# Loading and splitting the first two chunks of u at the point where the dense tokens are loaded

## Chip, core and metric

One NeuronCore of a Trainium2 chip runs the whole program in one launch. The metric is the device time in microseconds (us). The kernel before took 2869.16 us (median of three runs, 2865.69 to 2877.17).

## What is computed

One residual block on x of shape 1024 tokens by 1024, in float32. The part that matters here is its last third, the product-key expert layer:

```python
q = (xt @ w_query).reshape(T, 8, 2, 128)
s = einsum('thpd,hpkd->thpk', q, sub_keys)       # scores, 8 heads x 2 x 128 keys
# top 16 of each half, top 16 of their sums -> idx (T, 8, 16), gate = softmax
a = gelu(einsum('td,thkd->thk', xb, expert_u[idx]))
out = einsum('thk,thkd->td', a * gate, expert_v[idx])
```

There are 16384 experts, rows of u and v of 1024 numbers each. Ahead of it stand an RMS norm, the mLSTM and gMLP mixers and an output projection.

## The kernel before

**Two kinds of tokens.** The 1024 tokens are 8 blocks of 128. Blocks 0 to 4 are "dense": all 16384 experts are evaluated for them by matmuls, 128 chunks of 128 experts, and a matrix G holds the gate of each expert and token (zero for most). Blocks 5 to 7 are "sparse": for each of a token's 128 picked experts a row of u, later of v, is gathered by an indirect DMA that POOL issues, and DVE does a dot product or a weighted sum.

**The front.** `front_part` runs three times, over blocks 0-1, 2-4 and 5-7. Its last step is eight calls of `query` (L419): a weight load and split (`split_w`), 48 matmuls into `pq`, their copy on ACT, 12 matmuls of scores (`psc`, L444), and a store of the scores to DRAM that ACT's queue issues (L447, `d_sc<-sc`). The top-k steps load them back on SP's queue (L464, `scb<-d_sc`). Between these stand the gate units of the dense blocks (`gate_units`): DVE builds one-hot tiles `AB` (L656), ACT scales them (L659), PE multiplies them into `pG` (L661), ACT copies that to `Gt` (L662), and ACT's queue stores it to `d_G`.

**open_x.** In the third part, ahead of the eight queries, `open_x` (L738, called at L628) closes the pool of the mixers and opens the pool `xparts` in its place, at the right end of SBUF. It loads the dense tokens `xh` and `xl` (ten loads of 512 KB, L748). `xparts` also holds two buffers for raw chunks of u and v.

**The dense phase.** `experts` opens the pool `dense` where the pool of the front lay, so its tiles wait for the tiles of the front that they overlap. `stage1` takes a chunk of u: load to `raw` (L777), ACT copies it to `uhi` rounded to fp32r (L778), POOL subtracts to get `ulo` (L779). Then `mm3` does three matmuls (hi by hi, hi by lo, lo by hi) for each of 8 slices and each of two half-chunks of 320 tokens: 24 matmuls into one of three PSUM buffers `pa`. ACT takes the GELU (L787), DVE multiplies by the gates `Gin` (L789), ACT and DVE split into `wh` and `wl` (L790, L791), and only then is the `pa` buffer free. `Gin` is loaded once for four chunks (L771, 1280 KB). After four chunks `stage2` splits four chunks of v (L800 to L802), multiplies into `pout` and adds to `acc` (L816).

**Where a raw chunk goes.** `raw()` counts its calls. Until `experts` sets `dense_phase`, every raw tile comes from `xparts`; after that, calls number 1, 4, 5, 8, 9, ... come from the pool `dense`. So before the change the raw tile of chunk 0 lies in `dense`, those of chunks 1 and 2 in `xparts`, that of chunk 3 in `dense`.

**Order.** The code is written in program order, but a list scheduler with a simulated timeline decides the order of each engine's and queue's instructions: it takes the earliest in program order of those that it thinks are ready. Each engine and each queue then runs in that fixed order.

Of the kernel before, what the change touches and what calls it, by code (L numbers as in the profile page):

```python
# [7 lines left out]
F32 = mybir.dt.float32  # L8
F32R = mybir.dt.float32r
# [3 lines left out]
AF = mybir.ActivationFunctionType  # L13
OP = mybir.AluOpType
# [27 lines left out]
SLOW = 0  # L42
ORDER = [0, 1, 4, 2, 3, 5, 6, 7]
SPREAD = 0.96


class Build:
# [690 lines left out]
    def open_x(self):  # L738

        nc = self.nc  # L740
        self.cm.close()
        self.xp = self.ctx.enter_context(self.tc.tile_pool(name="xparts", bufs=1, side="right", reuse_waits="tile"))
        T = len(self.dense) * 128
        self.xh = self.xp.tile([128, 8, T], F32R, name="xh", tag="xh")
        self.xl = self.xp.tile([128, 8, T], F32R, name="xl", tag="xl")
        for s, blk in enumerate(self.dense):
            for src, dst in ((self.d_xh, self.xh), (self.d_xl, self.xl)):
                nc.sync.dma_start(dst[:, :, s * 128:(s + 1) * 128].bitcast(F32), src[blk])  # L748

    def raw(self):  # L750
        self.nraw += 1
        if self.dense_phase and self.nraw % (2 + NRAW2) < NRAW2:
            return self.dp.tile([128, D], F32, name="raw", tag="raw", bufs=NRAW2)
        return self.xp.tile([128, D], F32, name="raw", tag="raw", bufs=2)

    def experts(self, side, dp, ps):
        nc, v = self.nc, self.nc.vector
        self.dense_phase = True
        self.dp = dp
        xh, xl = self.xh, self.xl  # L760
        ND = len(self.dense)
        T = ND * 128
        T2 = T // 2
        n32 = T // TG
        ngroups = NEXP // GS
        W, V, st = {}, {}, {"n": 0}

        def stage1(g, e):
            if e == 0:
                st["G"] = dp.tile([128, n32, GS, TG], F32, name="Gin", tag="Gin", bufs=1)  # L770
                nc.sync.dma_start(st["G"], self.d_G[:, :, g * GS:(g + 1) * GS].rearrange("n j i t -> j n i t"))  # L771
            G = st["G"]
            i = g * GS + e
            ur = self.raw().rearrange("p (c j) -> p c j", c=8)
            ul = dp.tile([128, 8, 128], F32R, name="ulo", tag="ulo", bufs=2)
            uh = dp.tile([128, 8, 128], F32R, name="uhi", tag="uhi", bufs=2)
            nc.sync.dma_start(ur, self.I["uT"][i])  # L777
            nc.scalar.activation(uh, ur, AF.Copy)  # L778
            nc.gpsimd.tensor_tensor(ul, ur, uh.bitcast(F32), op=OP.subtract)  # L779
            wh = dp.tile([128, T], F32R, name="wh", tag="wh", bufs=GS + 1)  # L780
            wl = dp.tile([128, T], F32R, name="wl", tag="wl", bufs=GS + 1)
            for s in range(2):
                pa = ps.tile([128, T2], F32, name="pa", tag="pa", bufs=3)
                sl = slice(s * T2, (s + 1) * T2)
                self.mm3(pa, [((uh[:, c], ul[:, c]), (xh[:, c, sl], xl[:, c, sl])) for c in range(8)])
                with self.first():
                    nc.scalar.activation(pa, pa, AF.Gelu_apprx_tanh)  # L787
                    p3 = pa.rearrange("p (n t) -> p n t", t=TG)
                    v.tensor_tensor(p3, p3, G[:, s * (n32 // 2):(s + 1) * (n32 // 2), e], op=OP.mult)  # L789
                    nc.scalar.activation(wh[:, sl], pa, AF.Copy)  # L790
                    v.tensor_sub(wl[:, sl], pa, wh[:, sl].bitcast(F32))  # L791
            W[i] = (wh, wl)

        def stage2(g):
            vhs, vls = (self.gp.tile([128, GS, D], F32R, name=n, tag="Gt", bufs=2) for n in ("vhi", "vlo"))
            for e in range(GS):
                i = g * GS + e
                vr = self.raw()
                vh, vl = vhs[:, e], vls[:, e]
                nc.sync.dma_start(vr, self.I["v"][i * 128:(i + 1) * 128])  # L800
                nc.scalar.activation(vh, vr, AF.Copy)  # L801
                nc.gpsimd.tensor_tensor(vl, vr, vh.bitcast(F32), op=OP.subtract)  # L802
                V[i] = (vh, vl)
            for s in range(ND):
                for d in range(2):
                    if st["n"] % 3 == 0:
                        po = ps.tile([128, 512], F32, name="pout", tag="pout", bufs=1)
                    else:
                        po = self.gps.tile([128, 512], F32, name="pout", tag="pG", bufs=2)
                    st["n"] += 1  # L810
                    dl = slice(d * 512, (d + 1) * 512)
                    sl = slice(s * 128, (s + 1) * 128)
                    self.mm3(po, [((W[i][0][:, sl], W[i][1][:, sl]), (V[i][0][:, dl], V[i][1][:, dl]))
                                  for i in range(g * GS, (g + 1) * GS)])
                    with self.first():
                        v.tensor_add(st["acc"][:, s, dl], st["acc"][:, s, dl], po)  # L816

        for f in side:
            f()
        units = []  # L820
        for n in range(len(self.sparse)):
            steps = self.sparse_units(self.sparse[n], dp, ps)
            more = [f for b in self.sparse[n + 1:n + 2] for f in self.topk_units(b)]
            for q, f in enumerate(steps):
                units.append(f)
                if q % 20 == 19 and more:
                    units.append(more.pop(0))
            units += more
        last = units.pop()
        k = 0  # L830
        for g in range(ngroups):
            for e in range(GS):
                stage1(g, e)
                i = g * GS + e - LAG
                want = min(len(units), int(len(units) * (i + 1) / (SPREAD * (NEXP - LAG))))
                while k < want:
                    units[k]()
                    k += 1
            if g == 0:
                acc = dp.tile([128, ND, D], F32, name="acc", tag="acc")  # L840
                for s, blk in enumerate(self.dense):
                    nc.sync.dma_start(acc[:, s], self.d_x1[blk])
                st["acc"] = acc
            stage2(g)
        self.fg = dp.tile([128, D], F32, name="fgrow", tag="Gin", bufs=1)
        nc.sync.dma_start(self.fg, self.I["fg"].partition_broadcast(128))
        for s, blk in enumerate(self.dense):
            self.final(blk, acc[:, s], dp)
        for f in units[k:] + [last]:
            f()  # L850
# [148 lines left out]
```

## Time and profile before

| | us |
|---|---|
| median of three runs | 2869.16 |
| profiled execution, its own time | 2870.66 |
| profiled execution, first to last instruction (span) | 2868.9 |
| PE busy, of the span | 2707.1 (94%) |
| DVE busy | 2198.3 (77%) |
| POOL busy | 1498.8 (52%) |
| ACT busy | 1120.5 (39%) |

Matmul ends are modelled, so a busy PE is not a PE at its peak: counts and starts of matmuls tell its pace. The front ends and the dense phase begins at about 973 us of the span. In a timeline row, "0.42 PE ... [3.23 <-DVE acc L816]" means that the engine stood idle 3.23 us before this and that acc, written at line 816 on DVE, ended the wait. PE is the matmuls, PEld the weight loads beside them, SPq and ACTq the DMA queues of those engines.

### The profile page before, as it was taken

The numbers are of one execution on the slowest core, as the hardware profiler recorded it, in microseconds if no ns is written. First come the engines' busy times: TensorE is split into PE (matmuls) and PEld (weight loads), VectorE is DVE, ScalarE is ACT, GpSimd is POOL, SyncE is SP. The second block draws the span as 40 slices with busy tenths as digits, with TensorE's granted clock in tenths as the row PEclk, the third lists the DMA queues.
The fourth block names the chain that finished last, engine by engine and source line by source line (L and its number), as shares of the span: only waits on it lengthen the run. The fifth ranks groups of instructions, "written<-read, shape, count | busy, mean of one in ns | idle before, by whom it ended". The sixth has DMA issues, their size and how long they took to land.

```text
span 2868.9 us, 44783 instructions
## 1 busy us (share of the span) xinstructions
PE 2707.1 (94%) x16283; PEld 2468.9 (86%) x16283; DVE 2198.3 (77%) x4981; ACT 1120.5 (39%) x2295; POOL 1498.8 (52%) x1220
## 2 busy tenths in 40 slices
PE   7888989999898799999999999999999999999998
PEld 7887989889898798889888888888888898889987
DVE  6649975289985677888797787978987777777774
ACT  5444788348888322223222222222222222222222
POOL 4430020000200186767767677667767777777873
PEclk9989999999999899999999999999999999999999
DMA  7797557866578798988989999898989999999992
GB/s 252 253 315 281 187 216 278 277 223 226 186 274 312 257 328 299 335 313 311 326 282 331 338 322 330 300 344 302 316 284 342 343 330 332 331 322 326 336 320 111
DMA packets 327821, 838.41 MB, mean 292 GB/s; under 512 B 25520, under 2 KB 161072, under 8 KB 315824
## 3 DMA queue, kind: packets, MB, share of 16 engines
q0 software_dynamic: 114048, 427.87, 40.4%
q1 hardware_dynamic: 190544, 347.91, 37.0%
q10 hardware_dynamic: 23008, 59.77, 5.3%
q8 instruction: 128, 2.10, 0.3%
q14 instruction: 93, 0.76, 0.1%
HBM read 746.32 MB, written 89.13 MB: 291 GB/s over the span
## 4 chain that ended last, share of the span: by engine, by line
PE 58%; DVE 19%; DMA 9%; ACT 5%; issue 5%; POOL 3%; SPq 1%; ACTq 1%; another core or an unknown queue 0%; POOLq 0%; DVEq 0%
PE pa L96 8%; PE pa L94 7%; PE pa L95 7%; PE pout L94 7%; PE pout L95 7%; PE pout L96 7%; DMA Gin<-d_G 4%; DVE gat L697 2%; PE pG L661 2%; DVE sacc L713 2%; DVE AB L656 2%; PE pq L94 2%; PE pq L96 2%; PE pq L95 2%; DMA wraw<-win 1%
## 5 line engine op out<-in xcount | busy, mean ns | idle before, releaser
L94 PE MATMUL pa<-xh,uhi 128*128 128x320 f32 x2048 | 639.3, 312 | 28.9 <-ACT uhi L778 14.9
L95 PE MATMUL pa<-xl,uhi 128*128 128x320 f32 x2048 | 637.1, 311 | 0.0
L96 PE MATMUL pa<-xh,ulo 128*128 128x320 f32 x2048 | 625.5, 311 | 5.4 <-POOL ulo L779 5.4
L94 PE MATMUL pout<-vhi,wh 128*128 128x512 f32 x1280 | 505.4, 400 | 23.0 <-DVE acc L816 11.1
L713 DVE SCALAR_TENSOR_TENSOR sacc<-gat,aw,sacc 128x1024 f32<-128x1024 f32 x384 | 492.3, 1282 | 27.4 <-DMA gat<-v,ix 22.3
L95 PE MATMUL pout<-vlo,wh 128*128 128x512 f32 x1280 | 509.0, 399 | 0.0
L96 PE MATMUL pout<-vhi,wl 128*128 128x512 f32 x1280 | 490.2, 398 | 0.0
L709 POOL DMA_INDIRECT gat<-v,ix x384 | 363.5, 947 | 239.8 <-DVE sacc L713 131.0
L697 DVE SCALAR_TENSOR_TENSOR gat<-gat,xn 128x1024 f32<-128x1024 f32 x384 | 459.5, 1213 | 20.0 <-DMA gat<-u,ix 19.8
L693 POOL DMA_INDIRECT gat<-u,ix x384 | 363.3, 946 | 209.5 <-DVE gat L697 104.3
L94 PEld LDWEIGHTS pa<-xh,uhi 128*128 128x128 f32 x2048 | 389.2, 190 | 43.2 <-DVE wl L791 16.1
L96 PEld LDWEIGHTS pa<-xh,ulo 128*128 128x128 f32 x2048 | 385.7, 190 | 12.9 <-POOL ulo L779 8.2
L95 PEld LDWEIGHTS pa<-xl,uhi 128*128 128x128 f32 x2048 | 389.3, 190 | 7.3
L779 POOL TENSOR_TENSOR ulo<-raw,uhi 128x1024 fp32r<-128x1024 f32 x128 | 308.7, 2413 | 145.6 <-ACT uhi L778 142.9
L801 ACT ACTIVATE vhi<-raw 128x1024 fp32r<-128x1024 f32 x128 | 131.7, 1052 | 487.5 <-PE pout L95 414.8
L802 POOL TENSOR_TENSOR vlo<-raw,vhi 128x1024 fp32r<-128x1024 f32 x128 | 307.9, 2416 | 22.7 <-ACT vhi L801 20.3
L94 PEld LDWEIGHTS pout<-vhi,wh 128*128 128x128 f32 x1280 | 242.0, 190 | 78.8 <-DVE acc L816 14.4
L816 DVE TENSOR_TENSOR acc<-acc,pout 128x512 f32<-128x512 f32 x320 | 214.2, 682 | 113.8 <-PE pout L96 89.9
L96 PEld LDWEIGHTS pout<-vhi,wl 128*128 128x128 f32 x1280 | 241.0, 190 | 54.0 <-DVE wl L791 0.4
L95 PEld LDWEIGHTS pout<-vlo,wh 128*128 128x128 f32 x1280 | 242.9, 190 | 50.2
L789 DVE TENSOR_TENSOR pa<-pa,Gin 128x320 f32<-128x320 f32 x256 | 126.7, 495 | 191.5 <-ACT pa L787 104.9
L790 ACT ACTIVATE wh<-pa 128x320 fp32r<-128x320 f32 x256 | 111.6, 436 | 379.0 <-DVE pa L789 315.0
(243 smaller groups left out, 5037.8 us busy)
## 6 DMA issues: line engine op xcount, KB each, us to landing
raw<-uT SPq DMA_DIRECT2D x128, 512.0 KB
raw<-v SPq DMA_DIRECT2D x128, 512.0 KB
wlo<-d_wl SPq DMA_DIRECT2D x48, 1024.0 KB
d_G<-Gt ACTq DMA_DIRECT2D x20, 2048.0 KB
Gin<-d_G SPq DMA_DIRECT2D x32, 1280.0 KB
wraw<-win SPq DMA_DIRECT2D x72, 512.0 KB
d_wl<-wlo POOLq DMA_DIRECT2D x24, 1024.0 KB
wraw<-wq SPq DMA_DIRECT2D x48, 512.0 KB
```

Source lines behind the costliest of these rows:

```text
L94: te.matmul(ps, lh, rh, start=k == 0, stop=False)
L95: te.matmul(ps, lh, rl, start=False, stop=False)
L96: te.matmul(ps, ll, rh, start=False, stop=k == n - 1)
L693: gd = nc.gpsimd.indirect_dma_start(out=t, out_offset=None, in_=self.I["u"], in_offset=bass.IndirectOffsetOnAxis(ap=st["ix"][:, k:k + 1], ...
L697: v.scalar_tensor_tensor(t, t, 1.0, st["xn"], op0=OP.mult, op1=OP.mult, accum_out=st["a"][:, k:k + 1])
L709: gd = nc.gpsimd.indirect_dma_start(out=t, out_offset=None, in_=self.I["v"], in_offset=bass.IndirectOffsetOnAxis(ap=st["ix"][:, k:k + 1], ...
L713: v.scalar_tensor_tensor(st["acc"], t, st["a"][:, k:k + 1], st["acc"], op0=OP.mult, op1=OP.add)
L779: nc.gpsimd.tensor_tensor(ul, ur, uh.bitcast(F32), op=OP.subtract)
L789: v.tensor_tensor(p3, p3, G[:, s * (n32 // 2):(s + 1) * (n32 // 2), e], op=OP.mult)
L801: nc.scalar.activation(vh, vr, AF.Copy)
L802: nc.gpsimd.tensor_tensor(vl, vr, vh.bitcast(F32), op=OP.subtract)
L816: v.tensor_add(st["acc"][:, s, dl], st["acc"][:, s, dl], po)
```

## The change

Two chunks (AHEAD = 2) of u are loaded and split inside `open_x`, right behind the loads of the dense tokens. The buffers of the split u (`ulo`, `uhi`, two of 4 KB per partition each) move from the pool `dense` to the pool `xparts`. Since `dense_phase` is not yet set there, the raw tiles of chunks 0 and 1 both come from `xparts`; chunk 2 is then in `xparts` and chunk 3 in `dense`, as before. `Gin`, `wh`, `wl`, `acc` and the other raw tiles stay in `dense`.

```diff
+AHEAD = 2
@@ open_x
                 nc.sync.dma_start(dst[:, :, s * 128:(s + 1) * 128].bitcast(F32), src[blk])
+        self.U = {i: self.split_u(i) for i in range(AHEAD)}
+
+    def split_u(self, i):
+
+        nc = self.nc
+        ur = self.raw().rearrange("p (c j) -> p c j", c=8)
+        ul = self.xp.tile([128, 8, 128], F32R, name="ulo", tag="ulo", bufs=2)
+        uh = self.xp.tile([128, 8, 128], F32R, name="uhi", tag="uhi", bufs=2)
+        nc.sync.dma_start(ur, self.I["uT"][i])
+        nc.scalar.activation(uh, ur, AF.Copy)
+        nc.gpsimd.tensor_tensor(ul, ur, uh.bitcast(F32), op=OP.subtract)
+        return uh, ul
@@ stage1
-            ur = self.raw().rearrange("p (c j) -> p c j", c=8)
-            ul = dp.tile([128, 8, 128], F32R, name="ulo", tag="ulo", bufs=2)
-            uh = dp.tile([128, 8, 128], F32R, name="uhi", tag="uhi", bufs=2)
-            nc.sync.dma_start(ur, self.I["uT"][i])
-            nc.scalar.activation(uh, ur, AF.Copy)
-            nc.gpsimd.tensor_tensor(ul, ur, uh.bitcast(F32), op=OP.subtract)
+            uh, ul = self.U.pop(i) if i in self.U else self.split_u(i)
```

## Rows read from the trace of the kernel before

**Rows 1.** Windows, by stage: start and end in us, length, then busy time and instructions of each engine, granted PE clock, DMA share, GB/s.

```profile
900.00:973.00 73.00, 72.21 (x471) 71.64 (x469) 40.39 (x178) 43.00 (x103) 0.00 (x0) 0.98 0.72 262
973.00:988.00 15.00, 0.21 (x1) 0.21 (x2) 12.74 (x83) 1.91 (x4) 0.18 (x1) 0.59 0.77 237
988.00:996.00 8.00, 7.28 (x27) 6.88 (x28) 7.86 (x14) 2.12 (x3) 7.21 (x5) 0.50 1.03 405
996.00:1006.00 10.00, 10.00 (x69) 10.00 (x69) 5.71 (x14) 5.25 (x9) 6.85 (x6) 0.99 0.82 308
1112.00:2858.00 1746.00, 1707.52 (x9334) 1530.31 (x9333) 1396.09 (x2347) 452.44 (x746) 1256.49 (x969) 0.99 0.89 315
```

**Rows 2.** Timeline of PE around the end of the front.

```profile
971.01 1.90 PE L444 MATMUL psc<-kk,qk 128*128 128x128 f32 x12
987.79 0.63 PE L94 MATMUL pa<-xh,uhi 128*128 128x320 f32 x1 [14.89 <-ACT uhi L778]
...
990.48 0.63 PE L96 MATMUL pa<-xh,ulo 128*128 128x320 f32 x1 [0.72 <-POOL ulo L779]
...
1006.31 0.86 PE L94 MATMUL pout<-vhi,wh 128*128 128x512 f32 x3
```

**Rows 3.** The chain that ended last, in order of time, over the same stretch (start us, us, what).

```profile
976.68 0.39 SPq L771
977.12 9.54 DMA raw<-uT
```

**Rows 4.** Timeline of SP's queue (start us, us of the issue or of a run of issues, then count).

```profile
880.46 1.74 SPq L748 DMA_DIRECT2D xh<-d_xh  x1
...
886.96 0.90 SPq L777 DMA_DIRECT2D raw<-uT  x2
...
954.35 22.24 SPq L464 DMA_DIRECT2D scb<-d_sc  x4
976.68 0.39 SPq L771 DMA_DIRECT2D Gin<-d_G  x1
977.12 4.26 SPq L777 DMA_DIRECT2D raw<-uT  x2
981.42 3.20 SPq L842 DMA_DIRECT2D acc<-d_x  x5
```

**Rows 5.** PE's waits from 988 us to the end of the dense phase, by what it waited for (us in total, times, longest us).

```profile
PE pa L94 <- DVE wl L791: 11.5, 11, 2.3
PE pout L94 <- DVE acc L816: 11.1, 6, 3.2
PE pout L94 <- ACT wh L790: 11.0, 5, 5.2
```

**Rows 6.** Timeline of DVE: the first gate multiplication and the first `wl` of the dense phase.

```profile
996.99 0.50 DVE L789 TENSOR_TENSOR pa<-pa,Gin 128x320 f32<-128x320 f32 x1
997.99 0.49 DVE L791 TENSOR_TENSOR wl<-pa,wh 128x320 fp32r<-128x320 f32 x1 [0.50 <-ACT wh L790]
```

**Rows 7.** Windows of the same columns as in rows 1, for the stretch in which the first `Gin` was loaded.

```profile
978.00:984.00 6.00, 0.00 (x0) 0.00 (x0) 5.26 (x42) 0.00 (x0) 0.00 (x0) 0.50 0.96 232
984.00:987.00 3.00, 0.00 (x0) 0.00 (x0) 2.90 (x21) 0.32 (x1) 0.00 (x0) 0.50 1.02 408
```

**Rows 8.** The chain that ended last, at the third load of `Gin`.

```profile
1085.01 21.43 DMA Gin<-d_G
```

**Rows 9.** Timeline of PE at the same load: the last matmul ahead of the wait, the first behind it, one at the lower clock and one at the full clock again.

```profile
1104.24 0.40 PE L96 MATMUL pout<-vhi,wl 128*128 128x512 f32 x1
1107.86 0.50 PE L94 MATMUL pout<-vhi,wh 128*128 128x512 f32 x1 [3.23 <-DVE acc L816]
...
1109.02 0.63 PE L95 MATMUL pout<-vlo,wh 128*128 128x512 f32 x1
...
1112.31 0.39 PE L94 MATMUL pout<-vhi,wh 128*128 128x512 f32 x1
```

**Rows 10.** Timeline of POOL (first row of the dense phase, then the first and the last of the five gathers that follow).

```profile
987.82 4.93 POOL L779 TENSOR_TENSOR ulo<-raw,uhi 128x1024 fp32r<-128x1024 f32 x2 [140.86 <-ACT uhi L778]
992.92 1.09 POOL L693 DMA_INDIRECT gat<-u,ix  x1 [0.18 <-issue]
...
998.27 0.93 POOL L693 DMA_INDIRECT gat<-u,ix  x1 [0.30 <-issue]
```

**Rows 11.** Timeline of DVE: the write of the tokens `xn` that the first gathered rows are multiplied with.

```profile
974.78 1.28 DVE L688 SCALAR_TENSOR_TENSOR xn<-gat,rall 128x1024 f32<-128x1024 f32 x1
```

**Rows 12.** Timeline of ACT: its longest wait in the stretch of the queries (first two rows), and the splits of chunks 0 and 1, which the change moves (last row).

```profile
888.22 0.38 ACTq L447 DMA_DIRECT2D d_sc<-sc  x1
888.64 1.28 ACT L659 ACTIVATE AB<-AB,ijgT 128x128 f32<-128x128 f32 x4 [9.85 <-DMA xh<-d_xh]
...
986.68 2.00 ACT L778 ACTIVATE uhi<-raw 128x1024 fp32r<-128x1024 f32 x2 [13.09 <-DMA raw<-uT]
```

**Rows 13.** Windows of the same columns as in rows 1, for the ten us behind that wait.

```profile
890.00:900.00 10.00, 7.72 (x52) 7.53 (x53) 4.81 (x4) 10.00 (x29) 0.00 (x0) 0.81 1.02 402
```

**Rows 14.** Timeline of DVE: an operation (L525) with POOL idle and beside POOL's first split of u (last two rows), and a build of `AB` in the stretch of the queries (first row).

```profile
892.62 1.23 DVE L656 TENSOR_TENSOR AB<-iota,ijgT 128x1024 f32<-128x1024 f32 x1 [8.23 <-PE pG L661]
...
968.02 0.30 DVE L525 SCALAR_TENSOR_TENSOR rk<-cq,cu 128x64 bf16<-128x64 f32 x1
...
988.12 2.46 DVE L525 SCALAR_TENSOR_TENSOR rk<-cq,cu 128x64 bf16<-128x64 f32 x1
```

## The prediction

> **What bounds the kernel now.** I read the windows by stage first. From 900 to 973 us PE is busy 72.2 of 73.0 us, and from 1112 us to the end of the dense phase 1707.5 of 1746.0; DVE, the next, has 1396 of those 1746 [rows 1]. So PE sets the end, and a microsecond that PE gets back at the seam of the two stages should reach the end. The waits that PE has left in the dense phase (11.5, 11.1 and 11.0 us are the largest sums) hang on the pace of PE itself [rows 5].
>
> Between them is a hole: 973 to 988 us holds one matmul. The timeline of PE puts 14.89 us there, from the last scores (end 972.9) to the first `pa` matmul at 987.79, released by `uhi`, and another 0.72 us for `ulo` [rows 2]. Behind the hole the granted clock is 0.50 (1.2 GHz) until 996: 27 matmuls in 7.28 us of busy time, 0.270 us each, against 69 in 10.0 us, 0.145 each, once it is 0.99 [rows 1].
>
> The chain tells why `uhi` was late: SP issues `Gin` at 976.68 and the raw tile of chunk 0 at 977.12, and that load ends 9.54 us later [rows 3]. SP had issued two raw loads, chunks 1 and 2, at 886.96, but chunk 0 stands behind the wait of the score loads, which lasts to 976.6 [rows 4]. By the counter in `raw()`, chunk 0's tile is in the pool `dense`, over tiles that the queries still use; the split's buffers are there too.
>
> **What it removes.** Both splits' loads, ACT and POOL work then lie ahead of the last queries, in space that those don't use, and the hole's cause goes: 14.89 + 0.72 us of idle PE [rows 2] and the low clock behind it, 27 matmuls x (0.270 - 0.145) = 3.4 us. Ceiling: 19.0 us. Chunk 0's load joins its neighbours at 886.96, where chunk 2 stood; chunk 2 follows when chunk 0 is split. SP thus has one raw load less behind 976.68.
>
> **What is late next.** PE can do three half-chunks, one for each `pa` buffer: 3 x 24 x 0.145 = 10.4 us, to 983.3. The fourth needs a `pa` buffer back, so it needs `Gin`, and the change moves neither `Gin` nor what SP waits for ahead of it: issue at 976.68 [rows 4]. No row shows when it landed. Lower end: from 978 to 984 us the DMA engines moved 6 us x 232 GB/s = 1.39 MB, where `Gin` is 1.31 MB; 408 GB/s follow, as other loads do [rows 7]. So it had landed by about 984. Upper end: the third `Gin` took 21.43 us [rows 8], which here gives 998.1.
>
> The change itself pushes it off the lower end. POOL's first work in the dense phase was two splits, 4.93 us from 987.82, and five gathers behind them [rows 10]. With the splits gone, those gathers can start when `xn` is written, at about 976 [rows 11], and run beside `Gin`: 5 x 0.52 = 2.6 MB, 6.5 us at the 405 GB/s of the stretch where they ran before [rows 1]. I let two thirds of that delay `Gin` and take 988, nearer to the lower end because the third `Gin` had all the traffic of the running loop around it. The Trainium skill, DMA: Bandwidth & Descriptors, section Queues, rings and completion order, says that each DMA engine takes turns between queues with work, packet by packet. No row shows the turns; by that rule the gathers take half of the engines' time while both run, an estimate of 990 for `Gin` and 2 us less gain.
>
> From `Gin` to a free buffer are one gate multiplication, `wh` and `wl`: 996.99 to 998.48, 1.5 us [rows 6]. So the fourth half-chunk starts at 989.5, after 6.2 us of idle PE. A 3.23 us idle was enough to bring the clock down once: matmuls 0.43 us apart instead of 0.23 from 1109.0 to 1112.2 [rows 9], some 1.7 us lost. So I take all 24 matmuls at 0.270 = 6.5 us: end 996.0. Before, it ended where `pout` starts, 1006.3 [rows 2]. **Gain at the seam: 10.3 us.** With `Gin` at 984 the idle is 2.2 us, and the end 985.5 + 3.5 + 1.7 = 990.7: gain 15.6. With 998.1 it is 999.6 + 6.5 = 1006.1: gain 0.2.
>
> Behind that, chunks 2 and 3 and the first chunks of v come no later than before: POOL has 4.9 us less to do there, and `acc`'s five loads stand behind `Gin` as they did [rows 4]. I cost them at nothing; what hides them is the 14 us of matmuls for chunks 2 and 3, and without that cover a late split costs PE its 2.4 us.
>
> **What it adds ahead of the queries' end.** PE has no slack from 900 to 973, so a delay there counts in full.
> - ACT: two splits, 2.0 us [rows 12], in a stretch where ACT is busy 10.00 of 10.00 us and PE 7.72 [rows 13]. 0 to 2.0 us.
> - DMA: 1 MB that may come ahead of the queries' weights, at 402 GB/s [rows 13]: 0 to 2.6 us. In the trace the raw loads already stand among these weights, so nearer 0.
> - DVE beside POOL: POOL is idle for 140.86 us ahead of its first split [rows 10]. Beside that split, DVE's L525 took 2.46 us instead of 0.30 [rows 14]. In the query stretch DVE builds `AB` (1.23 us each), which PE's gate products wait for. Two delays of 2.16: 0 to 4.3 us. No row shows an `AB` beside POOL work. The Trainium skill, SBUF — State Buffer, section Who interferes with whom, says that a DVE instruction with two SBUF inputs and a GpSimd one that reads SBUF shut each other out for a whole instruction. That speaks against the change; `AB` has two such inputs, and by the rule the upper end of this term would stand, 3 us above what I take.
> - A wait: ACT stood idle 9.85 us until 888, at its store of scores, released by one of the token loads [rows 12]; that load was issued at 880.46 [rows 4]. Which load this store waits for may shift by one, 1.7 us by the issue of a load: -2 to +2 us.
>
> From -2 to +9 in all; I take 3, most of it ACT.
>
> **Sum.** -10.3 + 3 = -7.3 us on the profiled execution's own 2870.66 us (span 2868.9), so 2863.4. The median of the runs is 1.5 us lower, 2869.16: forecast 2862.
>
> **Rivals.**
> 1. *The full hole comes back.* `Gin` lands by 984, the new work ahead hides under ACT's 9.85 us wait [rows 12], or the scheduler lets `pa` matmuls fill the last gaps of the queries. For it: 1.39 MB in 6 us [rows 7]. Against: the gathers start with `Gin`. 2869.2 - 15.6 - 1.5 = 2852.
> 2. *The wait changes its name.* `Gin` takes the 21.4 us that it takes later [rows 8], and PE's hole is as long, now behind DVE L789. Gain 0.2, cost 3: 2872. It also comes about if `pa` matmuls run ahead of the last queries, as they then delay the release of `Gin`'s space.
> 3. *Slower: ACT is held in the queries.* ACT runs in order; if a split of u is placed ahead of `AB`, `Gt` or a copy of `pq`, it waits for a load that queues behind ten token loads of 0.5 MB, and ACT, which the trace already shows held until 888, is held longer. Each us goes to PE, which has none to spare until 973 [rows 1]. It decides from 10.3 us on: with ACT held until 896 (8 us), 2.0 for the splits, 4.3 for DVE and 2 of low clock it is 16.3, net +6, 2875; held ten us longer it is 2885. Against: the raw loads were issued within 7 us of the token loads, and 402 GB/s brings them in 2.6 us each pair.
> 4. *Nothing moves.* The scheduler keeps the two splits at the end of the queries, in its own order: 2869. Against: it already hoisted two raw loads to 886.96 [rows 4], and nothing is left that would hold their splits.
>
> **How the numbers follow.** Forecast 0.45, rivals 0.22, 0.18, 0.10 and 0.05. A measurement of this kernel can tell about 0.5%, 14.3 us, from no change: below 2854.8 lies most of rival 1 and a small part of the forecast's own spread, since the order of the dense phase is dealt anew and its 11 us waits [rows 5] may grow or shrink: 0.27. Above 2883.5 lies half of rival 3 and a little of the others: 0.09. Within: 0.64. The range takes the seam's ends and the added costs, cut to what 8 in 10 need: 2847 to 2877.
>
> **What would show it.** `uhi` and `ulo` of chunks 0 and 1 at 885 to 910 us of the span; the first `pa` matmul within 1 us of the last scores, at full clock; then one idle of 2 to 8 us on PE that ends with a `wl` whose gate multiplication waited for the DMA of `Gin`; gathers from about 976; the last scores 0 to 5 us later than 972.9. I am wrong if PE has no second hole, if that hole is over 12 us, if the queries end over 8 us late, or if the dense phase changes length by more than 8 us.

## The result and the profile after

The changed kernel took 2886.4 us (median of 11 runs) where the kernel before, run beside it, took 2869.4: a ratio of 1.0062, 95% interval 1.0041 to 1.0082. It is 12 to 24 us slower, outside the range that was forecast. A second measurement (a_again) gave 1.0069 (1.0043 to 1.0095). The profiled execution took 2881.0 us, its span 2879.0. That span is 10.1 us longer than the one that the forecast rests on, but 9.8 of these lie ahead of the end of the last scores (982.7 us against 972.9), in a front that differs from execution to execution: a second profile of the kernel before (b_again) has that end at 978.0. So one pair of profiles doesn't tell where the loss is.

**The seam.** Two groups answer to [rows 2] and [rows 1]. First the timeline of PE (start, us, engine, line, operation, idle time before it and who ended it), with the code of the front one line further down than before, that of the dense phase mostly eight:

```profile
980.79 1.90 PE L445 MATMUL psc<-kk,qk 128*128 128x128 f32 x12
982.45 0.39 PE L95 MATMUL pa<-xh,uhi 128*128 128x320 f32 x1
...
1005.97 0.64 PE L95 MATMUL pa<-xh,uhi 128*128 128x320 f32 x1 [12.72 <-DVE wl L799]
...
1030.71 0.80 PE L96 MATMUL pout<-vlo,wh 128*128 128x512 f32 x1 [4.01 <-POOL vlo L810]
1042.54 0.50 PE L96 MATMUL pout<-vlo,wh 128*128 128x512 f32 x1 [2.69 <-POOL vlo L810]
```

The first `pa` matmul follows the scores at once. The hole of 14.89 us is gone, and one of 12.72 stands ten microseconds further on, with two smaller ones behind it, where PE waits for the split of v (`vlo`). In the windows by stage (columns as in [rows 1]) PE is busy 1704.3 of the last one's 1746 us, against 1707.5 of as many before:

```profile
910.00:982.50 72.50, 71.80 (x470) 71.42 (x468) 41.69 (x174) 44.82 (x104) 5.50 (x2) 0.98 0.75 275
996.00:1006.00 10.00, 0.03 (x1) 0.03 (x1) 2.12 (x11) 1.20 (x3) 0.47 (x1) 0.50 1.04 398
1122.00:2868.00 1746.00, 1704.29 (x9344) 1529.37 (x9343) 1396.84 (x2355) 452.51 (x746) 1260.40 (x972) 0.99 0.90 315
```

The splits did move. Here are SP's raw loads and `Gin` [rows 4], ACT's `uhi` [rows 12], and POOL's splits and first gathers [rows 10]:

```profile
894.20 2.12 SPq L758 DMA_DIRECT2D raw<-uT  x2
...
986.43 0.39 SPq L784 DMA_DIRECT2D Gin<-d_G  x1
```

```profile
910.34 1.07 ACT L759 ACTIVATE uhi<-raw 128x1024 fp32r<-128x1024 f32 x1
912.93 1.08 ACT L759 ACTIVATE uhi<-raw 128x1024 fp32r<-128x1024 f32 x1
```

```profile
911.49 2.39 POOL L760 TENSOR_TENSOR ulo<-raw,uhi 128x1024 fp32r<-128x1024 f32 x1 [59.91 <-ACT uhi L759]
...
985.63 1.10 POOL L694 DMA_INDIRECT gat<-u,ix  x1 [68.43 <-DVE tv L555]
...
995.54 0.94 POOL L694 DMA_INDIRECT gat<-u,ix  x1 [0.30 <-issue]
1007.32 0.94 POOL L694 DMA_INDIRECT gat<-u,ix  x1 [10.85 <-DVE s L554]
```

What ends the new hole is in DVE's timeline (first row) and in the chain of waits (second):

```profile
1004.07 0.50 DVE L797 TENSOR_TENSOR pa<-pa,Gin 128x320 f32<-128x320 f32 x1 [7.88 <-DMA Gin<-d_G]
```

```profile
986.43 17.55 DMA Gin<-d_G
```

`Gin` took 17.55 us. Seven gathers were issued before it landed: five from 985.63 us on, two more from 994.27. In the DMA view of 986.4 to 1004 us the gathers' queue has 55.0% of the engines' time, the queue with `Gin` and all other loads 42.9%. DVE stood still in its fixed order, and behind the gate multiplication stood the rest of block 5's top-k, so POOL's next gathers came 10.85 us late, and the splits of v behind those.

**The dense phase.** PE's waits from 983 us on (compare [rows 5]):

```profile
PE pa L95 <- DVE wl L799: 27.4, 10, 12.7
PE pout L95 <- DVE acc L824: 15.9, 5, 4.8
PE pout L96 <- POOL vlo L810: 6.7, 2, 4.0
PE pa L97 <- POOL ulo L760: 6.7, 8, 2.2
```

The time between certain additions into `acc` (320 in all, ten for each group of four chunks) shows where they matter. All times of this kind, here and below, count from the start of the last matmul of scores to the start of the addition. "Before" has two profiles, the one that the forecast rests on and the run b_again; "after" has two as well.

| us | last score to 20th addition | to 80th | 80th to 240th | 240th to 320th | last score to end |
|---|---|---|---|---|---|
| before | 144.4 / 141.7 | 501.7 / 492.4 | 928.7 / 922.0 | 455.9 / 450.8 | 1896.3 / 1875.2 |
| after | 146.7 / 147.6 | 490.5 / 490.9 | 949.9 / 944.4 | 446.2 / 446.1 | 1896.6 / 1891.3 |

The seam gained nothing, and 16 to 28 us are lost between the 80th and the 240th addition, 500 to 1400 us behind the seam; 7 to 14 us come back ahead of that stretch (20th to 80th) and 5 to 10 behind it. In the stretch PE stands idle 35.6 and 32.6 us in the two profiles of after, 22.5 and 18.2 in those of before. One of the new holes, in PE's timeline, with DVE's timeline and the chain of waits for its cause:

```profile
1650.76 0.79 PE L95 MATMUL pout<-vhi,wh 128*128 128x512 f32 x1 [4.79 <-DVE acc L824]
```

```profile
1647.48 0.50 DVE L797 TENSOR_TENSOR pa<-pa,Gin 128x320 f32<-128x320 f32 x1 [7.05 <-DMA Gin<-d_G]
```

```profile
1627.01 20.37 DMA Gin<-d_G
```

DVE waits in order for `Gin`; the additions that would free `pout`'s buffer stand behind it. Waits of DVE for `Gin` are not new (in that stretch 28.0 and 26.0 us in after, 24.8 and 17.6 in before): what stands behind them is. The second profile of after has the same hole (5.23 us), both come right behind the 106th addition, and neither profile of before has one over 0.8 us from 1600 to 1680 us.

### The profile page after: what moved, and what is told of

Same layout as the page of the kernel before. It is cut to its first block, busy times and chain, and to the rows that moved or that the text cites. A ratio compares the mean times of both kernels' runs of the same rounds, so it can differ in the third digit from the quotient of the medians.

```text
span 2879.0 us, 44766 instructions
## 1 busy us (share of the span) xinstructions
PE 2708.5 (94%) x16283; PEld 2469.8 (86%) x16283; DVE 2202.2 (76%) x4981; ACT 1122.0 (39%) x2297; POOL 1499.5 (52%) x1220
## 4 chain that ended last, share of the span: by engine, by line
PE 63%; DVE 14%; DMA 9%; ACT 5%; issue 4%; POOL 3%; SPq 1%; ACTq 1%; POOLq 0%; DVEq 0%
PE pout L95 8%; PE pout L96 8%; PE pout L97 8%; PE pa L97 8%; PE pa L95 8%; PE pa L96 8%; PE pG L662 3%; DMA Gin<-d_G 3%; DVE gat L698 2%; PE pq L95 2%; PE pq L97 2%; PE pq L96 2%; DMA raw<-v 1%; ACT AB L660 1%; DVE AB L657 1%
## 5 line engine op out<-in xcount | busy, mean ns | idle before, releaser
L97 PE MATMUL pout<-vhi,wl 128*128 128x512 f32 x1280 | 490.5, 399 | 0.0
L96 PEld LDWEIGHTS pout<-vlo,wh 128*128 128x128 f32 x1280 | 244.0, 191 | 59.4 <-POOL vlo L810 7.6
L797 DVE TENSOR_TENSOR pa<-pa,Gin 128x320 f32<-128x320 f32 x256 | 126.8, 495 | 162.8 <-ACT pa L795 110.7
## 6 DMA issues: line engine op xcount, KB each, us to landing
d_G<-Gt ACTq DMA_DIRECT2D x20, 2048.0 KB, 10.1
Gin<-d_G SPq DMA_DIRECT2D x32, 1280.0 KB, 13.8
```

The source lines that it names most:

```text
L96: te.matmul(ps, lh, rl, start=False, stop=False)
L97: te.matmul(ps, ll, rh, start=False, stop=k == n - 1)
```

## The experiments

All ratios are to the kernel before on the same chip, with 95% intervals.

**a_again**: the changed kernel, unaltered.

> The changed kernel once more, unaltered, for a second profile. In the first pair of profiles the token loads (SP, xh<-d_xh) already start 9.3 us later (863.7 before, 873.0 after), although every engine's instruction order up to there is the same; from there to the end the two differ by 1.1 us only. Theory A (the 9.3 us is what one execution of the front differs from another): here the token loads start anywhere from 860 to 876, and the stretch from them to the end of the span is 2006 us again, within 4. Theory B (something in the changed kernel slows the front every time): they start at 870 to 876 again, and the whole gap of the medians, 17 us, is to be split between this and the dense phase.

1.0069 (1.0043 to 1.0095). The loss is real, and the holes of the first profile stand again in the same groups. The token loads start at 873.6 us, as theory B had it, and the span ends 1999.5 us later, which theory A (2006, within 4) didn't allow. Part of those 9 us is the front after all (b_again), part the place of `xh` (ahead0).

**ahead0**: only the buffers move. The order of the instructions on every engine is that of the kernel before.

```diff
-AHEAD = 2
+AHEAD = 0
```

> AHEAD = 0: the split's buffers lie beside the dense tokens as in the changed kernel, but nothing is loaded or split there; the order on SP and POOL at the seam is that of the kernel before. Theory 1 (the loss comes from the splits' new place: Gin's load then runs beside the gathers, and the order behind it is another): the time is that of the kernel before, ratio 0.997 to 1.003, the hole on PE is 14.9 us behind the scores and ends with uhi. Theory B (the new addresses alone cost, in the front or in the dense phase): ratio 1.004 to 1.008 as for the changed kernel.

1.0025 (1.0011 to 1.004), with the old hole (14.13 us, released by `uhi`): theory 1's range, but the interval leaves out 1. So places alone cost something, 3 to 11 us. Why is in the chains of waits ahead of the loads of `xh`, in the kernel before and in the changed one:

```profile
862.97 0.68 PE tp L108 x6
863.65 0.02 SPq L748
863.67 0.03 issue
863.71 0.62 SPq L748
```

```profile
871.83 0.49 ACT Gt L663
872.33 0.62 DVE al L119
872.97 0.61 SPq L749
```

`xparts` grew by 16 KB at its lower end, so `xh` starts that much lower. By the kernel's text it used to lie over `nat`, last read by PE's transposes, and now covers the norm's gain `n2g` too, which DVE reads until its last `al`. The loads wait for it, and the queries' weights stand behind them on SP. Counted from the 128th split of a weight chunk on ACT, the loads start 45.5 to 46.8 us later in ten profiles with `xh` at its old place and 48.8 to 50.2 in seven with the new one; the scores end 152.4 to 155.0 and 156.4 to 159.6 us later. The means differ by 3.4 us.

**nog0**: the first group's products are multiplied by a slice of `xh`, and its `Gin` is not loaded (the kernel leaves out the gates of four chunks).

```diff
-            if e == 0:
+            if e == 0 and g:
...
+                    gs = G[:, s * (n32 // 2):(s + 1) * (n32 // 2), e] if g else xh[:, e, sl].bitcast(F32).rearrange("p (n t) -> p n t", t=TG)
+                    v.tensor_tensor(p3, p3, gs, op=OP.mult)
```

> The changed kernel, but the first four chunks are multiplied by a slice of xh instead of by the gates, so they wait for no load of Gin (part of the result is left out in that way). Theory 1 (Gin's landing is the bound that took the place of the hole, 12.7 us of PE's and 7.9 us of DVE's waiting, with what queues behind them on DVE): the hole of 12.7 us goes, no idle over 4 us on PE until 1020 us, and the time is 12 to 20 us under the changed kernel's, ratio to the kernel before 0.998 to 1.003. Theory 2 (the loss is in the rest of the dense phase or in the front, not at the seam): the hole goes, but the time stays within 5 us of the changed kernel's, ratio 1.004 to 1.008.

1.0033 (1.002 to 1.0046), between what the two theories gave. Without the load the 12.72 us are down to 2.57: `Gin` is what ended that hole. But the waits for `vlo` grow from 6.7 to 10.1 us, in PE's timeline:

```profile
1023.59 0.50 PE L96 MATMUL pout<-vlo,wh 128*128 128x512 f32 x1 [3.52 <-POOL vlo L811]
1032.55 0.80 PE L96 MATMUL pout<-vlo,wh 128*128 128x512 f32 x1 [6.59 <-POOL vlo L811]
```

In POOL's order gathers stand ahead of these splits, and the one at 1020.22 us waited 4.35 us for DVE's top-k. So the 10th addition comes 76.6 us after the scores, no earlier than in the kernel before (77.4, 76.1), though earlier than the 83.2 of the changed kernel.

**lag4**: the sparse rows start three chunks later.

```diff
-LAG = 1
+LAG = 4
```

> The changed kernel with LAG = 4: the first gathers come behind the fourth chunk, so none runs beside the first load of Gin; the gathers behind are paced 2.4% denser. Gin lands when the first multiplication by it starts: 17.55 us after its issue in the changed kernel. Theory 1a (the gathers slow Gin): it takes 7 to 11 us here and the hole on PE is 2 to 6 us. Theory 1b (Gin is slow by itself, or by the raw and acc loads on its own queue): still 14 to 18 us and a hole of 9 us or more. The total is not a clean measure, as the gathers' pace changes: expected within 15 us of the changed kernel.

1.0035 (1.001 to 1.006). `Gin` lands 8.2 us after its issue, by the DMA view, instead of 17.55, and the hole is 3.98 us: theory 1a. So the gathers had held `Gin` up. The other profiles agree: 7.8 to 8.3 us in the eight that show its landing and have no gather beside it, 14.7 to 18.4 in the six with five to seven. By the 80th addition nothing of that is left (492.7 us, before 492.4 and 501.7).

**b_again, a_bord2, b_aord2, a_bord**: is it the order? Each is one of the two kernels with edges added to the scheduler's input that fix the order of issue on all five engines, and take nothing else away. In the name, the first letter is the kernel (a is the changed one), "bord" and "aord" the kernel whose order is imposed, and 2 means from the 20th addition on.

```diff
+            if prev is not None:
+                tc.add_manual_dep(by[e][k], prev, mybir.DependencyInfo(
+                    mybir.DependencyClass.NoSync, mybir.DependencyReason.DATA), reason="order")
+            prev = by[e][k].name
```

> The kernel before, unaltered. Ratio 1.000, with an interval that shows what two equal kernels differ by here (0.998 to 1.002 expected). Its profile tells whether the loads of xh start at 863.7 us, as in the first profile of this kernel, or at 873 to 875 us, as in the four profiles of kernels whose instructions up to that point are the same on every engine. Theory A (the front varies from execution to execution): 870 to 876 us now, with the end moved by as much less whatever the dense phase gains. Rival (the first 870 us really are shorter in this kernel, by its addresses): 862 to 866 us again, and then about 10 us of the loss of the changed kernel lie ahead of the change.

> The changed kernel, with the order of the instructions on all five engines pinned to that of the kernel before from the 20th addition into acc on; up to there its own order stands. Theory A (the change costs because the order of the whole dense phase was dealt anew, some 14 to 20 us between the 80th and the 240th addition, and 2 to 6 us at the seam): 2865 to 2872 us, ratio 1.000 to 1.003, and the stretch from the 80th to the 240th addition takes 925 to 935 us instead of 944 to 950. Rival (the loss is made by addresses and by transfers that meet otherwise, not by the order): ratio 1.005 to 1.009 as for the changed kernel, the stretch 942 to 950 us.

> The kernel before, with the order of the instructions on all five engines pinned to that of the changed kernel from the 20th addition into acc on; its seam, its loads and its buffers are its own. Theory A: the order alone costs what the changed kernel lost, ratio 1.004 to 1.008, and the stretch from the 80th to the 240th addition takes 942 to 952 us, with holes of 3 to 5 us in PE's work in the same groups. Rival: ratio 0.999 to 1.002, the stretch 925 to 935 us.

> The changed kernel, with the order of all five engines pinned to that of the kernel before throughout, the seam too: only the two loads and the four splits of u stand earlier, and the buffers lie as in the changed kernel. Theory A: the seam's hole is set by Gin here as well, since Gin is issued as late and the five gathers run beside it: the first gate multiplication comes 15 to 20 us after Gin is issued, PE's largest hole at the seam is 8 to 13 us, and the time is 2862 to 2870 us, ratio 0.999 to 1.003. Rival (without the new order the change gives what I took for its seam, 7 to 10 us): ratio 0.9955 to 0.998, holes at the seam below 5 us.

| | seam, places | order from the 20th addition | ratio | 80th to 240th |
|---|---|---|---|---|
| b_again | before | before | 0.9985 (0.9961 to 1.0009) | 922.0 us |
| b_aord2 | before | after | 1.0034 (1.001 to 1.0058) | 954.8 us |
| a_bord2 | after | before | 1.0049 (1.0027 to 1.0072) | 924.1 us |
| a_bord | splits and places of after, whole order of before | before | 1.0007 (0.9983 to 1.0031) | 923.3 us |

b_again shows what equal kernels differ by; its token loads start at 869.9 us, so the front varies (863.7 in the first profile of the same kernel). The kernel before with nothing changed but the order behind the 20th addition is slower by 3 to 17 us, with after's pace (954.8 us) and a hole of 4.55 us released by `acc` behind the same 106th addition as in the changed kernel. So the stretch follows the order. a_bord2 was to be at 1.000 to 1.003 and was not: the stretch is back to 924.1 us, but the total isn't. Its 20th to 80th addition takes 360.0 us, where the same order behind its own seam takes 350.7 and 357.3: the joint seems to cost 3 to 9 us. b_aord2's joint shows no such cost (343.8 us, as in the changed kernel). With before's order throughout (a_bord) the loss is within the noise, so the order as a whole carries it, and the edges that fix it cost nothing that shows. a_bord was to show a hole set by `Gin`; the hole is there (9.91 us), and `Gin` landed at 999.35 us, but DVE had no wait for it: it came to the first gate multiplication at 999.87, at the end of 14 us of top-k work. In before's order the top-k on DVE is a bound as late as `Gin`.

**a_xlow_bord**: as a_bord, with the four split buffers below `xh`, so that `xh` lies as before.

```diff
+        pre = [self.parts_u() for i in range(AHEAD)]
         self.xh = self.xp.tile([128, 8, T], F32R, name="xh", tag="xh")
...
+        self.U = {i: self.split_u(i, pre[i]) for i in range(AHEAD)}
```

> As a_bord (the changed kernel, order of all five engines pinned to that of the kernel before), with the four buffers of the split u placed below xh and xl, so that xh, xl and the raw buffers lie where they lie in the kernel before, and no longer over the norm's gain n2g. Theory A (part of the loss is where xh lies: its loads wait for the last al on DVE, which reads n2g, and no longer for the last transpose on PE): the first load of xh comes 45 to 47 us after the 120th split of a weight chunk on ACT, as in the three profiles with xh at its old place (45.5, 46.8, 45.5), not 49 to 50 us as in the seven others; the scores end 154 to 155 us after it, not 156.5 to 159.6; the time falls by 2 to 5 us against a_bord, ratio 0.997 to 1.000. Rival (the loads of xh don't hold the queries up; the place is without effect): scores' end 157 to 159 us after that split, ratio 1.000 to 1.002.

1.0008 (0.9986 to 1.0031). The text says the 120th split; its figures are those of the 128th. From that one the loads of `xh` start after 46.8 us and the scores end after 152.4, so the trace has the gain. The times don't show it (1.0008 against a_bord's 1.0007): 3 us is less than these intervals tell. The seam, in PE's timeline:

```profile
998.23 0.64 PE L242 MATMUL pa<-xh,uhi 128*128 128x320 f32 x1 [9.99 <-DVE wl L953]
1007.75 1.65 PE L242 MATMUL pout<-vhi,wh 128*128 128x512 f32 x3 [3.55 <-ACT vhi L963]
1011.13 0.63 PE L242 MATMUL pa<-xh,uhi 128*128 128x320 f32 x1 [1.74 <-DVE wl L953]
```

15.3 us of idle time in three pieces, where the kernel before has 15.6 in two [rows 2].

**a_best**: also, the gates of the first two chunks come by loads of their own into the raw buffers, some 20 us ahead of the scores' end. Before's order from the 20th addition on.

```diff
+            Ge.append(self.xp.tile([128, n32, TG], F32, name="Ge", tag="raw", bufs=2))
...
+                d = nc.sync.dma_start(Ge[e], self.d_G[:, :, e].rearrange("n j t -> j n t"))
```

> As a_xlow_bord, but the order is pinned to that of the kernel before only from the 20th addition into acc on, and the gates of the first two chunks come by two loads of their own into the two raw buffers beside the dense tokens, long before the scores end; Gin is still loaded whole, and its first use is at the third chunk. Theory A (at the seam the early splits were worth nothing because Gin was the next bound, and the rest was order and place): PE runs the four halves of the first two chunks without waiting, the largest hole at the seam is below 6 us, and the 10th addition into acc comes 64 to 72 us after the scores' end (77 before, 83 in the changed kernel); 2850 to 2860 us, ratio 0.994 to 0.998. Rival (another wait stands right behind Gin, the top-k on DVE or the third chunk's u): a hole of 8 us or more remains, the 10th addition comes 74 us or more after the scores' end, ratio 0.998 to 1.003.

1.0037 (1.0017 to 1.0057): the rival. PE runs all four half-chunks without a wait and then stands still longer than ever:

```profile
1006.71 1.65 PE L171 MATMUL pout<-vhi,wh 128*128 128x512 f32 x3 [16.28 <-ACT vhi L893]
```

It waits for the first load of v (and the third chunk's u), which come in the same traffic. The windows of 25 us that start 5 us after the scores' end show it, in b_again, the changed kernel and a_best (the last two columns are the DMA engines' busy share and GB/s):

```profile
983.00:1008.00 25.00, 14.42 (x82) 14.02 (x83) 21.25 (x88) 8.26 (x12) 13.42 (x9) 0.69 1.00 356
```

```profile
987.00:1012.00 25.00, 12.28 (x74) 12.02 (x73) 15.43 (x71) 3.94 (x7) 8.97 (x8) 0.73 1.02 365
```

```profile
981.00:1006.00 25.00, 9.43 (x65) 9.17 (x63) 22.45 (x98) 4.67 (x10) 3.13 (x4) 0.74 0.99 356
```

The DMA engines are full, about 9 MB in 25 us, in all three. The two splits' loads are 1 MB of it; with them taken out other transfers come forward (gathers: 2.59 MB in b_again, 3.78 in the changed kernel). A full window alone doesn't tell that PE waits, though: nog0's is as full (share 1.04), with PE busy 21.63 of the 25 us, and its waits come behind it.

**b_defer, a_defer, a_best2**: the kernel before, a_xlow_bord's splits and a_best, each with the first gathers issued behind the fourth split of u and the loads of `acc` behind the fourth load of v; before's order from the 20th addition on. a_best2 has the third and fourth chunk's u in the dense pool.

```diff
+        tc.add_manual_dep(b.gathers[0], b.ulos[3].name, late, reason="order")
+        for x in b.accs:
+            tc.add_manual_dep(x, b.vraws[3].name, late, reason="order")
```

> The kernel before, with two changes of order only: the first gathers of the sparse rows are issued behind the split of the fourth chunk's u on POOL, and the five loads of acc behind the fourth load of v on SP; from the 20th addition into acc on the order is pinned to that of the kernel before. Theory A (from about 5 us after the scores' end until 25 to 30 us after it the DMA engines are full in every kernel so far, so what PE waits for there is set by the traffic in that stretch, some 9 MB, and not by two splits): the hole ahead of the first pa stays near 14 us, but the first group's ending comes earlier, the 10th addition 66 to 72 us after the scores' end (76 to 77 in the kernel before), and the time falls to 0.996 to 0.999 of the kernel before. Rival (the transfers are not what holds the first group): the 10th addition 75 to 78 us after the scores' end, ratio 0.999 to 1.002.

> The changed kernel with xh, xl and raw at their old places (as a_xlow_bord) and the same two changes of order as b_defer; from the 20th addition on the order of the kernel before. Theory A: with the traffic out of the way Gin lands about 9 us after its issue, as in lag4, the hole at the seam falls to 3 to 6 us, the 10th addition comes 60 to 68 us after the scores' end, ratio 0.994 to 0.997, and below b_defer by 3 to 8 us: so much the early splits are worth where Gin and the rest can follow. Rival: still a hole of 9 us or more at the seam, ratio 0.999 to 1.002, equal to b_defer within 2 us.

> As a_best (the gates of the first two chunks come by loads of their own ahead of the scores' end), with the same two changes of order as b_defer, and the third and fourth chunk's u in the two raw buffers of the dense pool. Theory A: no hole above 4 us at the seam, the 10th addition 58 to 66 us after the scores' end, ratio 0.993 to 0.9965. Rival: the third chunk's u lands as late as in a_best (hole of 12 us or more), ratio 0.999 to 1.003.

b_defer 1.0034 (1.0011 to 1.0057), a_defer 0.9995 (0.9974 to 1.0016), a_best2 0.9985 (0.9962 to 1.0007). a_defer's window and its largest hole, then a_best2's:

```profile
983.00:1008.00 25.00, 18.50 (x114) 17.98 (x112) 23.98 (x82) 9.02 (x14) 14.99 (x8) 0.86 0.80 276
```

```profile
995.03 0.64 PE L172 MATMUL pa<-xh,uhi 128*128 128x320 f32 x1 [6.15 <-DVE wl L885]
```

```profile
996.72 0.42 PE L172 MATMUL pa<-xh,uhi 128*128 128x320 f32 x1 [2.42 <-DVE wl L890]
```

With room on the DMA engines (0.80) the early splits do what they were to do: the 20th addition comes 126.8 and 126.1 us after the scores, against 141.7 and 144.4 before, and a_defer's interval lies below b_defer's median. b_defer itself gained nothing at the 10th addition (78.1 us), although its window is at a share of 0.66: the hole of 14.40 us behind `uhi` stands, so without early splits PE waits for u whatever else is moved. It takes both. But the 15 us are not in the ratio, and none of the three came to the ratio that its theory A gave. By the 40th addition a_defer is at 260.3 and a_best2 at 268.8 us, before at 267.6 and 260.5.

**a_best2_80, a_best2_free**: a_best2 with before's order only from the 80th addition on, and with none.

> As a_best2, with the order pinned to that of the kernel before only from the 80th addition into acc on, so that the order behind the seam may follow the earlier start. Theory A (a_best2 has the 20th addition 126 us after the scores' end where the kernel before has 142, and gives 15 us back by the 40th because the pinned order expects rows whose gathers were issued later): the 40th addition comes 245 to 260 us after the scores' end, not 269 as in a_best2, the 80th 478 to 490 (492 to 502 in the kernel before), ratio 0.994 to 0.998. Rival (what the seam gains is given back whatever the order, since the gathers left out of the seam have to be made up by DMA queues that are nine tenths full all through the dense phase): the 80th addition 490 us or more after the scores' end, ratio 0.998 to 1.002.

> As a_best2, with nothing pinned: the order is dealt anew over the whole dense phase. Theory A: a fourth order, whose pace between the 80th and the 240th addition may be anything from 922 us (as in the kernel before) to 955 us (as in the changed kernel); ratio 0.994 to 1.006. Rival (the pace depends on places and transfers, not on the order): 922 to 930 us as in a_best2 (925), ratio 0.997 to 1.000.

0.9998 (0.9979 to 1.0016) and 0.9985 (0.9967 to 1.0003). With the order free behind the seam the gain lasts: 244.0 and 245.0 us at the 40th addition, 480.1 and 481.6 at the 80th, there 11 to 22 ahead of before. Then a_best2_80 loses it (80th to 240th: 949.3 us), most of it where the two orders meet, in PE's timeline:

```profile
1476.29 0.79 PE L165 MATMUL pout<-vlo,wh 128*128 128x512 f32 x1 [10.80 <-POOL vlo L893]
1486.92 0.80 PE L164 MATMUL pout<-vhi,wh 128*128 128x512 f32 x1 [6.84 <-ACT wh L881]
```

a_best2_free loses it in its own deal, spread over the stretch from the 80th to the 240th addition: 944.9 us, like after. So up to the 80th addition the gathers that were put off cost nothing, and what gives the gain back behind it is the order or the joint of two, as far as these two runs tell; that it is the gathers' making up is not ruled out. That such a seam could keep its 11 us under an order as good as before's was not shown. No version here beats the kernel before beyond its interval.

## Why the prediction was wrong

**Right.** The first `pa` at the scores' heels and at full clock, the splits of u ahead of the last queries (910 to 917 us), a second hole that ends with a `wl` behind `Gin`, the gathers beside `Gin`. The queries kept PE busy (71.8 of 72.5 us), though ACT's wait there was 13.69 us instead of 9.85. One build of `AB` beside POOL's first split took nearly three times as long, in DVE's timeline:

```profile
910.12 1.22 DVE L657 TENSOR_TENSOR AB<-iota,ijgT 128x1024 f32<-128x1024 f32 x1 [1.61 <-ACT AB L660]
911.61 3.35 DVE L657 TENSOR_TENSOR AB<-iota,ijgT 128x1024 f32<-128x1024 f32 x1 [0.27 <-PE pG L662]
```

That agrees with what the Trainium skill says in SBUF — State Buffer, Who interferes with whom: the two shut each other out. PE's busy share in that stage shows no cost of it.

**The step on what is late next** failed. `Gin`'s landing was put at 988 with an issue at 976.68, 11 us, from bytes over a rate with a part of the gathers beside it. It took 17.55 us, nearer to the upper end of 21.4, and 8.2 with the gathers postponed: the two thirds of the gathers' time that were to delay it were too few. The estimate by the rule of turns, 990, was low as well. I read one load at a time, where [rows 1] had the whole stage at a DMA share of 1.03 behind 988 us. The step also let DVE come to the gate multiplication as soon as `Gin` lands. In the kernel before DVE has no wait ahead of that row [rows 6]: it comes there at 996.99, straight from the top-k, long after `Gin` could have landed by the forecast. With that order and the early splits it still comes there 19.6 us after the scores' end (a_bord). The hole was rival 2's, 12.72 us and 6.7 more at `vlo`; the gain of 10.3 us at the seam came out as a loss of 2 to 6 us at the 20th addition.

**"Chunks 2 and 3 and the first chunks of v come no later than before"** failed: DVE stood behind `Gin` with the top-k, and `vlo` followed late (4.01 and 2.69 us of PE; 10.1 us in nog0, where `Gin` is gone).

**The queries' 3 us** were the right size by luck. None of the four terms shows: with the early splits but `xh` at its old place (a_xlow_bord, a_defer, the a_best kernels) the scores end 152.4 to 155.0 us after the 128th split of a weight chunk, without the early splits 154.0 to 154.9. It was the place of `xh` over `n2g`, 3.4 us in the traces. A move of buffers was not costed at all.

**The rest of the dense phase** was left as a spread of both signs. Its waits were taken to hang on PE's own pace; the hole behind the 106th addition hangs on DVE behind a load of `Gin`, as the one in [rows 8] and [rows 9] did. It was the largest term: the order behind the 20th addition alone, in a kernel otherwise that of before, costs 0.34% (0.1 to 0.58), 3 to 17 us; and with the order of before throughout, the same splits and places cost nothing that shows (a_bord). By the sum of what was measured apart, 3.4 for the place, 2 to 6 at the seam and 10 for the order make 15 to 19 of the 18 to 20 us that the two ratios give; with the interval of the order's term that agreement is partly luck. a_bord2 (14 us where the same sum gives 5 to 9) has a joint of two orders on top. Why the dealt order is the worse one is shown at single holes only.

Of the forecast's own conditions for being wrong, a second hole over 12 us was met by 0.7 us, and the stretch from the 80th to the 240th addition alone grew by 16 to 28 us. Over the whole, from the last score to the end, four pairs of profiles differ by -5 to 21 us: there the condition can't be judged.

## What to carry to other kernels

A hole at a seam can have several bounds of nearly the same length. Here moving two loads ahead of a full stage renamed the wait, moving only the other traffic out of the stage left the first hole as it was, and the two together gained 15 to 18 us by the 20th addition. So ask of each next bound, a load, its neighbours on the DMA engines and the work ahead of it in its engine's order, when it would end if the first were gone. Where a scheduler deals the order, an edit in one place deals all of it anew; imposing the old order on the new kernel, and the new order on the old one, tells the edit's own worth from that of the deal. And a buffer that moves changes what its load waits for: look at which last reader lies under it.

## What was unexpected of the hardware

The same 1.31 MB load, the first `Gin`, landed 7.8 to 8.3 us after its issue without gathers and 14.7 to 18.4 us after it with five to seven of them. Over all groups of the changed kernel such a load takes 8.2 to 25.7 us, the median being 13.8; the hole at 1650.76 had one of 20.37. Beside that one the gathers' queue and the one with all the loads held nearly equal shares of the engines' time, in the DMA view of 1620 to 1650 us of the changed kernel (packets, MB, share of 16 engines):

```profile
q0 software_dynamic: 1305, 4.75, 43.7%
q1 hardware_dynamic: 3439, 4.43, 42.5%
```

The Trainium skill, DMA: Bandwidth & Descriptors, section Queues, rings and completion order, has each engine take turns between queues packet by packet. The two queues' shares of time are nearly equal here and 55.0% to 42.9% at the first `Gin`, but the packets that the profile counts are not (1305 against 3439), so no run here shows the turns themselves. What the runs show is that gathers held about half of the engines' time in both stretches, and that the first `Gin` took about twice as long beside them.

The front's first 820 us differ by up to 7 us between executions of the same instructions (the 128th split of a weight chunk comes at 818.2 to 825.2 us in the 17 profiles, taken on several chips), more than some of the parts that were to be told apart here; two profiles of the kernel before alone differ by 4.9 us there. Profiles were compared from the last score on for that reason.
